# Attention on TensorE: values of two key tiles on two halves of the columns, weights summed beside

## The chip, the cores and the metric

The kernel runs on one NeuronCore of a Trainium2 chip. A core has five engines with their own instruction streams: TensorE (PE) multiplies matrices into PSUM, VectorE (DVE), ScalarE (ACT) and GpSimd (POOL) work element by element, SyncE (SP) issues DMAs. They wait for each other through semaphores. The metric is the device time of one execution in microseconds (us); the kernel before takes 3555.32 us, the median of three runs (3553.36 to 3558.95).

## The reference

Two layers of a model over 1024 latent tokens and 256 context tokens. Each layer projects its input, runs four mixers side by side (a gated linear recurrence called mLSTM, attention, and two state-space mixers), projects their outputs back and ends with a feed-forward part. The change touches the attention alone, and there what stands behind the projections, the product of weights and values and the softmax's denominator:

```python
def attend(q, k, v):
    s = jnp.einsum('bqhd,bkhd->bhqk', q, k).astype(jnp.float32) * scale
    p = jax.nn.softmax(s, axis=-1).astype(v.dtype)
    return jnp.einsum('bhqk,bkhd->bqhd', p, v)
...
yc = attend(qc, kc, vc).reshape(bsz, Tc, W_GROUP)
...
k_all = jnp.concatenate([kl, kc], axis=1)
v_all = jnp.concatenate([vl, vc], axis=1)
```

There are 4 heads with 96 features for the scores and 64 for the values. Context queries see the 256 context keys, latent queries all 1280 keys.

## The kernel before

Activations lie feature-major: 128 features on the partitions, tokens along the row. Tokens come in groups t0 = 0 (256 context tokens), 256 and 768 (512 latent tokens each); the last layer leaves the first group out as queries. Dense products run in float32r, a form of float32 that PE takes in one pass, three times with split operands (L242 to L244, a_pkn among them for the keys); products marked float32 take two passes, and the trace shows each pass as an instruction of its own.

Attention (class MLA) first builds values and keys. `values` makes `vt`, the values of a 128-token tile, token-major, with a block of ones between the two heads of a pair. `attend` goes over two head pairs, the two heads of each, and the groups of queries. For a head and a group it goes over the key tiles, 10 for latent queries and 2 for context queries: three float32r products give the scores of 128 keys and up to 512 queries in a PSUM bank (pst, L934 to L936), ACT takes the exponential into a tile E (L938), and one float32 product of 128 columns (L939) adds to the bank po: 64 columns are the values, the other 64 are ones, so that po holds the weighted values on one half of its partitions and the sums of the weights on the other. Over both layers there are 160 such key tiles of 512 queries and 8 of 256. At the group's end ACT copies both halves out (L941, L942); after the second head of a pair DVE takes the reciprocal (L944), POOL multiplies (L945), and the result goes to DRAM.

Between these steps `extra()` puts in other work by a written plan: steps of the mLSTM mixer (`cell`, products L740, L745, L753, L778, the norm m_w and m_h on POOL at L773 and L774) and parts of the modulation vectors (L151, narrow products of 32 columns on the four quarters of PE's columns). `scores` makes the next head's keys and each query's largest score (L903, reduced on DVE at L904). The program is written in this order, but a scheduler with a model of the engines then sets the order in which each engine's instructions stand; every engine starts its own in that order.

PSUM has 8 banks: 2 for dense products (pd), 3 (pa) for attention's po and pst, 3 (pb) for the other strand. L702 (mLSTM states, ahead of attention) are float32 products of 64 columns whose outputs go alternately to partitions 0 to 63 and 64 to 127 of a tile. L183 (norms) are products of 32 columns.

Of the kernel before, what the change touches and what calls it, by code (L numbers as in the profile page):

```python
# [15 lines left out]
P = 128  # L16
# [10 lines left out]
# order of the 128-column tiles of w_in  # L27
# [3 lines left out]
# columns of the per-layer vector pack  # L31
# [24 lines left out]
# before attend, then before and after each group  # L56
# [7 lines left out]
class Kern:  # L64
# [10 lines left out]
    # ------------------------------------------------------------------ setup  # L75
    def setup(self):
# [34 lines left out]
        # two banks for the dense products, and three for each of two strands of other work  # L111
# [4 lines left out]
    def few(self):  # L116
        """the dense products keep to their two banks"""
        self.cycle, self.turn = [self.pd], 0

    def many(self):  # L120
        """the dense products take those of the second strand too"""
        self.cycle, self.turn = [self.pd, self.pb, self.pb, self.pd, self.pb], 0
# [6 lines left out]
    # --------------------------------------------------------- modulation vectors  # L129
# [7 lines left out]
    def mod(self, l, tiles_, ws, pool, bank=None):  # L137
        """c @ w_mod + b for some of the 48 tiles of 128 columns: the vectors are the stationary operand, with
        two tiles of rows on each of the four column groups."""
# [32 lines left out]
    # --------------------------------------------------------------------- norms  # L172
    def rstd(self, tiles, nfeat, n, pool, name, bufs=2, out=None, sqs=None):
        """1/sqrt(mean of squares over the features) for n tokens, on every partition."""
# [24 lines left out]
    def split(self, src, hi, lo, eng=None):  # L199
        """hi = src in float32r, lo = src - hi (exact)."""  # L200
        nc = self.nc
        nc.scalar.copy(hi, src)  # L202
        (eng or nc.gpsimd).tensor_tensor(lo, src, hi.bitcast(F32), OP.subtract)  # L203

    def norm_apply(self, l, which, k, x, rb, act, t0, n, pool):
        """act(hi, lo)[k][:, t0:t0+n] = x*rb*(1+scale)+shift."""
# [15 lines left out]
    # --------------------------------------------------------------------- dense  # L222
# [14 lines left out]
    def dense_acc(self, ps, whi, wlo, ahi, alo, ks, start=True, stop=True):  # L237
        """ps += sum_k w[k]^T a[k], three float32r passes. whi/wlo/ahi/alo: callables k -> AP."""
# [16 lines left out]
    def dense_late(self, srcs, act, early, late, chunks, evacs, pool, names):  # L255
        """dense for some tiles of columns, first over the rows that are there, then over those that come late"""
# [24 lines left out]
def pieces(t0, n):  # L281
    """cut a token range at the end of the context"""
    if t0 < TC < t0 + n:
        return [(t0, TC - t0), (TC, t0 + n - TC)]
    return [(t0, n)]


def ppos(t):
    """position of a token in a row padded with one zero before, between and behind"""
    return t + 1 if t < TC else t + 2  # L290
# [6 lines left out]
# ------------------------------------------------------------------------ gates  # L297
class Gates:
    """Per-token scalars of the two gated mixers, token-major [128, direction, chunk, head]."""

    def __init__(self, K, l, misc, keep, pool):
# [14 lines left out]
        # softplus of -f and of dt: max(z, 0) + log1p(exp(-|z|))  # L316
# [22 lines left out]
        # L[d, 0] = log forget gate, L[d, 1] = dt * A  # L339
# [34 lines left out]
    def mlstm(self, keep, pool):  # L374
# [12 lines left out]
        # running maximum of a within each chunk, along the direction's time  # L387
# [13 lines left out]
        # m over the chunks: m <- max(m, cmax) + total, from zero, in each direction's order  # L401
# [5 lines left out]
        def orders(dst, src, inv):  # L407
            # src [p, d, (c h)], dst [p, d, h, 11]
# [40 lines left out]
        # decay by head pair: the first 64 partitions carry the even head of a pair, the others the odd one  # L449
# [8 lines left out]
class Expo:  # L458
    """E[s, h, t] = exp(bias[s, h] + row[t, h]) for s at or before t in direction d, else 0. The exponent is a product
    of bfloat16 matrices: bias and row come in three exact parts each."""  # L460

    def __init__(self, K, l, name, bias, row, pool):
        """bias, row: [P, 2, 40] contiguous, token-major; row None: minus the bias"""
# [60 lines left out]
# -------------------------------------------------------------------------- SSD  # L524
def cslice(c):
    """columns of a 128-token chunk in a row that has one spare column behind the context"""
    t = c * P + (1 if c >= TC // P else 0)
    return slice(t, t + P)


def nexts():
    """nexts[d][c]: the chunk whose starting state chunk c completes in direction d"""
    return [{o[i]: o[i + 1] for i in range(NCH - 1)} for o in ORDER]


class SSD:
    """states(): convolution and the state before each chunk; outputs(): the rest. src(i): the six tiles x, B, C before the
    convolution, DRAM. zsrc: silu(z), DRAM. keep: holds the states."""

    def __init__(self, K, l, g, src, zsrc, oc, keep):  # L540
# [4 lines left out]
        # [n, chunk, group, direction, (head, p)]: state before the chunk  # L545
        self.S = keep.tile([P, NCH, 2, 2, P], F32, name=n("S"))
        # by chunk: B and C feature-major, x token-major
# [55 lines left out]
    def outputs(self, pb, y_put):  # L603
# [5 lines left out]
        for t0, w in groups:  # L609
            yz = pb.tile([P, 2, 512], F32, tag="yz", name=n(f"yz{t0}"))  # L610
            for c in range(t0 // P, (t0 + w) // P):
# [9 lines left out]
                px = K.pa.tile([P, 2, 2, 2, 64], F32, tag="m", name=n(f"px{c}"))      # [t, group, direction, head, p]  # L621
# [34 lines left out]
def conv3(nc, dst, src, w0, w1, w2, bias, n):  # L656
    """dst[0..n) = w0*src[0..n) + w1*src[1..n+1) + w2*src[2..n+2) + bias; the weights are per-partition scalars."""
# [8 lines left out]
# ------------------------------------------------------------------------ mLSTM  # L666
# [6 lines left out]
def mlstm_states(K, l, g, src, pool, tmp):  # L673
    """src(tile): DRAM, two feature-major tiles each of q, k (already times 1/8), v, sigmoid(o).
    Returns the state before each chunk and the values, token-major with a one behind each head, DRAM."""
# [3 lines left out]
    # state before each chunk, rows (head of the pair, dim): [., chunk, pair, direction, e|n]  # L679
# [36 lines left out]
def mlstm(K, l, g, src, oc, states, pool, y_put):  # L716
# [3 lines left out]
    # queries of the four heads, the rows of the other head of the pair zero  # L720
# [7 lines left out]
    for ci, c in enumerate(oc):  # L728
# [7 lines left out]
        u = pool.tile([P, 2, 4, 65], F32, tag="u", name=n(f"u{c}"), bufs=3)      # [t, direction, head, e|n]  # L736
        for q in range(2):
            px = K.psm.tile([P, 2, 2, 65], F32, tag="m", name=n(f"px{c}{q}"))      # [t, odd, direction, e|n]
# [46 lines left out]
# -------------------------------------------------------------------------- MLA  # L785
def latent_norms(K, l, src, dst, pool, groups_kv, groups_q):
    """rmsnorm of the compressed keys and values, dst[0], and of the compressed queries, dst[1:3]"""
# [12 lines left out]
class MLA:  # L800
    """queries(), values(): queries, values and keys; attend(): the rest. src(tile, i), lat: DRAM, feature-major."""
# [10 lines left out]
    def latents(self, pq):  # L812
        """loads ahead of queries()"""
# [5 lines left out]
    def queries(self, late, pool):  # L819
        K, l, n, lat, pq, ws = self.K, self.l, self.n, self.lat, self.pq, self.ws  # L820
        nc, A = K.nc, K.A
        # late holds what the last head needs too
# [19 lines left out]
    def values(self, late, pool, pk):  # L842
# [3 lines left out]
        vt = self.vt = late.tile([P, NCH, 2, 192], F32, name=n("vt"))       # values of a pair of heads with ones between  # L846
# [12 lines left out]
        # values, token-major  # L859
        wv = pk.tile([P, 256], F32, name=n("wv"))  # L860
        nc.sync.dma_start(wv, A["w_uv"][l])
        nc.gpsimd.memset(vt[:, :, :, 64:128], 1.0)
        for c in range(NCH):
            ps = K.acc(n(f"pv{c}"))
            nc.tensor.matmul(ps[:, :256], kvf[:, c * P:c * P + P], wv, start=True, stop=True)
            psv = ps[:, :256].rearrange("p (a h e) -> p a h e", a=2, h=2)
            for o in range(2):
                nc.scalar.copy(vt[:, c, :, 128 * o:128 * o + 64], psv[:, :, o])
        # rope part of the keys, on partitions 64-127 twice (it meets q*cos and swapped q*sin)
# [11 lines left out]
        # row 96 takes the largest score off  # L881
# [3 lines left out]
    def scores(self, h, pool):  # L885
        """keys of a head, and the largest score of each query, from the leading halves"""
# [24 lines left out]
    def attend(self, pool, epool, y_put, extra):  # L911
        K, groups, n = self.K, self.groups, self.n
        nc, vt = K.nc, self.vt
        scale = 96 ** -0.5
        self.scores(0, pool)
        for hp in range(2):
            ys = {}
            for ho in range(2):
                h = 2 * hp + ho
                kh, kl, qh, ql = self.kh[ho], self.kl[ho], self.qh[h], self.ql[h]  # L920
                if h < 3:
                    self.scores(h + 1, pool)
                for t0, w in groups:
# [4 lines left out]
                    # sums over the keys: the weighted values on one half of the partitions, the weights on the other  # L928
                    po = K.psm.tile([P, 512], F32, tag="m", name=n(f"po{h}{t0}"))
                    kts = range(2) if t0 < TC else range(NCH)  # L930
                    for kt in kts:
                        ks = slice(kt * P, kt * P + P)
                        ps = K.psm.tile([P, 512], F32, tag="m", name=n(f"pst{h}{t0}{kt}"))
                        nc.tensor.matmul(ps[:, :w], kh[:97, ks], qh[:97, t0:t0 + w], start=True, stop=False)  # L934
                        nc.tensor.matmul(ps[:, :w], kh[:96, ks], ql[:96, t0:t0 + w], start=False, stop=False)
                        nc.tensor.matmul(ps[:, :w], kl[:96, ks], qh[:96, t0:t0 + w], start=False, stop=True)  # L936
                        E = epool.tile([P, 512], F32, tag="E", name=n(f"E{h}{t0}{kt}"), bufs=3)
                        nc.scalar.activation(E[:, :w], ps[:, :w], AF.Exp, scale=scale)  # L938
                        nc.tensor.matmul(po[:, :w], vt[:, kt, hp, 64 * ho:64 * ho + P], E[:, :w], start=kt == 0, stop=kt == kts[-1])  # L939
                    me, ot = slice(64 * ho, 64 * ho + 64), slice(64 - 64 * ho, 128 - 64 * ho)  # L940
# [892 lines left out]
```

## Time and profile before

| what | value |
|---|---|
| runs | 3553.36, 3555.32, 3558.95 us |
| span of the profiled execution | 3550.2 us (its time outside the span is not given) |
| PE busy | 96% of the span |
| DVE, ACT, POOL busy | 48%, 31%, 25% |
| attention, layer 0 | 592 to 870 us |
| attention, layer 1 | 2448 to 2690 us |

The profile is of one execution; its times are in us from the start of the span, and Lnn is a line of the kernel. Products on PE are pipelined and their ends are modelled, so the time that a product costs is better read from the distance between starts than from its own length. Of a piece of several merged instructions the length goes from the first one's start to the last one's end.

### The profile page before, as it was taken

To read this page: it belongs to the slowest core of one execution; us is meant where nothing else is said; L and a number is where in the kernel's file an instruction comes from. 1 tells how busy PE (TensorE), PEld (TensorE's weight loads), DVE (VectorE), ACT (ScalarE), POOL (GpSimd) and SP (SyncE) were. 2 spreads that over 40 slices of the span, in tenths; PEclk is the share of its full clock that TensorE was granted. 3 is DMA by queue.
4 is the path that set the end of the run, shared out by engine and by line. 5 is a ranking of instruction groups with operands and counts; after the bars stand their busy time and mean duration, and the time that the engine had idled before them with its cause. 6 is when DMAs were issued, how large, how long until landed. Compare 5 with 4: busy or idle time off the path is not lost. (4 is left out here: it accounts for less than half of the span.)

```text
span 3550.2 us, 48986 instructions
## 1 busy us (share of the span) xinstructions
PE 3418.2 (96%) x19154; PEld 2795.2 (79%) x19186; DVE 1708.2 (48%) x3597; ACT 1106.9 (31%) x1885; POOL 889.9 (25%) x1061
## 2 busy tenths in 40 slices
PE   8899998999999999999999999998999999999998
PEld 6888995676768888888887889985666688888885
DVE  6857727554365486333323563636633432232333
ACT  4224534334242211111223324533333312212222
POOL 1922424011033222222221011331110223323321
PEclk9899998999999999999999999998999999999999
DMA  5577533345111121111112655542153111111111
GB/s 200 166 205 229 156 119 113 110 140 212 65 46 62 54 90 72 36 36 36 42 40 81 162 166 164 142 150 67 60 204 107 42 42 54 53 42 54 48 46 62
DMA packets 264904, 352.84 MB, mean 99 GB/s; under 512 B 89240, under 2 KB 190304, under 8 KB 264672
## 3 DMA queue, kind: packets, MB, share of 16 engines
q1 hardware_dynamic: 168148, 265.90, 23.5%
q10 hardware_dynamic: 96524, 83.81, 7.5%
q8 instruction: 151, 2.47, 0.3%
q14 instruction: 81, 0.66, 0.1%
HBM read 266.09 MB, written 83.52 MB: 98 GB/s over the span
## 5 line engine op out<-in xcount | busy, mean ns | idle before, releaser
L1601 DVE SCALAR_TENSOR_TENSOR x<-pd,modv,x 128x512 f32<-128x512 f32 (+1 forms) x448 | 299.8, 687 | 233.6 <-PE pd L244 233.2
L242 PE MATMUL pd<-fh,wh_d 128*128 128x512 f32 (+1 forms) x896 | 325.3, 369 | 9.3 <-ACT fh L202 5.7
L242 PE MATMUL ps_g<-hb,wh_g 128*128 128x512 f32 (+1 forms) x880 | 326.0, 370 | 3.2 <-ACT hb L214 2.2
L244 PE MATMUL ps_g<-hb,wl_g 128*128 128x512 f32 (+1 forms) x880 | 324.4, 369 | 2.5 <-POOL wl_g L203 2.5
L243 PE MATMUL pd<-fl,wh_d 128*128 128x512 f32 (+1 forms) x896 | 326.0, 367 | 0.7 <-POOL fl L203 0.7
L244 PE MATMUL pd<-fh,wl_d 128*128 128x512 f32 (+1 forms) x896 | 325.5, 368 | 0.0
L242 PE MATMUL ps_u<-hb,wh_u 128*128 128x512 f32 (+1 forms) x880 | 325.4, 370 | 0.0
L243 PE MATMUL ps_g<-hb,wh_g 128*128 128x512 f32 (+1 forms) x880 | 325.1, 369 | 0.0
L243 PE MATMUL ps_u<-hb,wh_u 128*128 128x512 f32 (+1 forms) x880 | 324.7, 369 | 0.0
L244 PE MATMUL ps_u<-hb,wl_u 128*128 128x512 f32 (+1 forms) x880 | 324.3, 369 | 0.2 <-POOL wl_u L203 0.2
L662 DVE SCALAR_TENSOR_TENSOR cv<-gp,vec,cv 128x1281 f32<-128x1281 f32 (+1 forms) x44 | 72.6, 1651 | 476.8 <-ACT cv L659 476.8
L242 PE MATMUL ps_in<-ha,wh_in 128*128 128x384 f32 (+3 forms) x688 | 218.3, 326 | 13.5 <-ACT st L1426 13.5
L203 POOL TENSOR_TENSOR wl_u<-wr_u,wh_u 128x1024 fp32r<-128x1024 f32 x44 | 105.5, 2397 | 481.7 <-ACT wh_u L202 481.7
L243 PE MATMUL ps_in<-ha,wh_in 128*128 128x384 f32 (+3 forms) x688 | 222.4, 323 | 0.0
L244 PE MATMUL ps_in<-ha,wl_in 128*128 128x384 f32 (+3 forms) x688 | 221.2, 322 | 0.0
L242 PE MATMUL ps_in<-hb,wh_in 128*128 128x256 f32 (+1 forms) x704 | 212.7, 305 | 0.8 <-ACT hb L214 0.6
L244 PE MATMUL ps_in<-hb,wl_in 128*128 128x256 f32 (+1 forms) x704 | 212.8, 303 | 0.0
L243 PE MATMUL ps_in<-hb,wh_in 128*128 128x256 f32 (+1 forms) x704 | 212.5, 302 | 0.2 <-DVE hb L215 0.2
L242 PEld LDWEIGHTS pd<-fh,wh_d 128*128 128x128 f32 x896 | 169.1, 189 | 45.8 <-DVE x L1601 7.4
L202 ACT CAST wh_u<-wr_u 128x1024 fp32r<-128x1024 f32 x44 | 46.3, 1051 | 502.4 <-PE pd L243 436.5
L242 PEld LDWEIGHTS ps_g<-hb,wh_g 128*128 128x128 f32 x880 | 166.2, 189 | 36.4 <-ACT hb L214 3.5
L243 PEld LDWEIGHTS pd<-fl,wh_d 128*128 128x128 f32 x896 | 169.4, 189 | 31.9 <-issue 1.7
(509 smaller groups left out, 7691.2 us busy)
## 6 DMA issues: line engine op xcount, KB each, us to landing
wm<-in_w_mod SPq DMA_DIRECT2D x96, 512.0 KB
wr_in<-in_w_in SPq DMA_DIRECT2D x44, 512.0 KB
wr_g<-in_w_up SPq DMA_DIRECT2D x44, 512.0 KB
wr_u<-in_w_up SPq DMA_DIRECT2D x44, 512.0 KB
wr_d<-in_w_down SPq DMA_DIRECT2D x44, 512.0 KB
wr_out<-in_w_out SPq DMA_DIRECT2D x32, 512.0 KB
PF<-st ACTq DMA_DIRECT2D x100, 128.0 KB
PF<-st ACTq DMA_DIRECT2D x60, 192.0 KB
```

The costliest lines, as they stand in the source:

```text
L202: nc.scalar.copy(hi, src)
L203: (eng or nc.gpsimd).tensor_tensor(lo, src, hi.bitcast(F32), OP.subtract)
L242: nc.tensor.matmul(ps, whi(k), ahi(k), start=start and i == 0, stop=False)
L243: nc.tensor.matmul(ps, whi(k), alo(k), start=False, stop=False)
L244: nc.tensor.matmul(ps, wlo(k), ahi(k), start=False, stop=stop and i == len(ks) - 1)
L662: nc.vector.scalar_tensor_tensor(dst, src[:, 0:n], w0, dst, OP.mult, OP.add)
L1601: nc.vector.scalar_tensor_tensor(v, ps, K.modv[l][:, 8 * part + m, c:c + 1], v, OP.mult, OP.add)
```

## The change

`vt` loses its ones and holds four heads of 64 columns. In `attend` the key tiles are taken two at a time. Their two value products are 64 columns wide and go to the two halves of po, the even key tile to partitions 0 to 63, the odd one to 64 to 127, both accumulated over the pairs; in the program they stand behind the score products of the next pair. The sums of the weights are formed apart: POOL adds the E tiles of the even key tiles, DVE those of the odd ones, DVE adds the two (tot), and one full-width float32 product with a matrix of ones (L976, `finish`) gives the sum over the partitions; it is put off until the next group's second pair. At the group's end ACT copies one half of po and DVE adds the other to it. E has six buffers instead of three.

```diff
-        vt = self.vt = late.tile([P, NCH, 2, 192], F32, name=n("vt"))       # values of a pair of heads with ones between
+        vt = self.vt = late.tile([P, NCH, 4, 64], F32, name=n("vt"))
...
-        nc.gpsimd.memset(vt[:, :, :, 64:128], 1.0)
         for c in range(NCH):
             ps = K.acc(n(f"pv{c}"))
             nc.tensor.matmul(ps[:, :256], kvf[:, c * P:c * P + P], wv, start=True, stop=True)
-            psv = ps[:, :256].rearrange("p (a h e) -> p a h e", a=2, h=2)
-            for o in range(2):
-                nc.scalar.copy(vt[:, c, :, 128 * o:128 * o + 64], psv[:, :, o])
+            nc.scalar.copy(vt[:, c], ps[:, :256].rearrange("p (h e) -> p h e", h=4))
...
-                    po = K.psm.tile([P, 512], F32, tag="m", name=n(f"po{h}{t0}"))
-                    kts = range(2) if t0 < TC else range(NCH)
-                    for kt in kts:
-                        ks = slice(kt * P, kt * P + P)
...
-                        E = epool.tile([P, 512], F32, tag="E", name=n(f"E{h}{t0}{kt}"), bufs=3)
-                        nc.scalar.activation(E[:, :w], ps[:, :w], AF.Exp, scale=scale)
-                        nc.tensor.matmul(po[:, :w], vt[:, kt, hp, 64 * ho:64 * ho + P], E[:, :w], start=kt == 0, stop=kt == kts[-1])
...
+                    po = bank(f"po{h}{t0}")
+                    nk = 2 if t0 < TC else NCH
+                    sums, old = [None, None], None
+
+                    def values(k0, es):
+                        for i, E in enumerate(es):
+                            nc.tensor.matmul(po[64 * i:64 * i + 64, :w], vt[:, k0 + i, h], E[:, :w], start=k0 == 0, stop=k0 + 2 == nk)
+
+                    for k0 in range(0, nk, 2):
+                        es = []
+                        for i in range(2):
...
+                            E = epool.tile([P, 512], F32, tag="E", name=n(f"E{h}{t0}{kt}"), bufs=6)
+                            nc.scalar.activation(E[:, :w], ps[:, :w], AF.Exp, scale=scale)
+                            es.append(E)
+                        if old:
+                            values(*old)
+                        if k0 == 2:
+                            settle()
+                        old = k0, es
+                        eng = (nc.gpsimd, nc.vector)
+                        for i, E in enumerate(es):
+                            if k0:
+                                new = epool.tile([P, 512], F32, tag=f"S{i}", name=n(f"S{i}{h}{t0}{k0}"), bufs=1) if k0 == 2 else sums[i]
+                                eng[i].tensor_tensor(new[:, :w], sums[i][:, :w], E[:, :w], OP.add)
+                                sums[i] = new
+                            else:
+                                sums[i] = E
+                    values(*old)
+                    tot = epool.tile([P, 512], F32, tag="S", name=n(f"S{h}{t0}"), bufs=1)
+                    nc.vector.tensor_tensor(tot[:, :w], sums[0][:, :w], sums[1][:, :w], OP.add)
                     nc.scalar.copy(r[me, :w], po[ot, :w])
-                    nc.scalar.copy(y[me, :w], po[me, :w])
...
+                    nc.vector.tensor_tensor(y[me, :w], po[me, :w], r[me, :w], OP.add)
+
+                    def finish(h=h, ho=ho, t0=t0, w=w, y=y, r=r, me=me, hp=hp, tot=tot):
+                        ps = bank(f"pr{h}{t0}")
+                        nc.tensor.matmul(ps[:, :w], K.ones, tot[:, :w], start=True, stop=True)
+                        nc.scalar.copy(r[me, :w], ps[me, :w])
+                        if ho:
+                            nc.vector.reciprocal(r[:, :w], r[:, :w])
+                            nc.gpsimd.tensor_tensor(y[:, :w], y[:, :w], r[:, :w], OP.mult)
+                            y_put(2 + hp, 1, y[:, None, :w], t0, w)
+
+                    settle()
+                    later.append(finish)
                     extra()
+        settle()
```

The scheduler sets the order anew. The next two pieces are of PE in layer 0 (a0), head 0, queries from 768 on; a name like E07683 is head 0, queries 768, key tile 3, and po0768 the bank of that head and group. Before, around the value products of key tiles 3 and 4:

```order
L939 MATMUL a0_po0768_7771<-a0_E07683_7797,a0_vt_6556 128x512
L934 MATMUL a0_pst07685_7807<-a0_qh0_6644,a0_kh0_6552 128x512
L935 MATMUL a0_pst07685_7807<-a0_ql0_6648,a0_kh0_6552 128x512
L936 MATMUL a0_pst07685_7807<-a0_qh0_6644,a0_kl0_6554 128x512
L939 MATMUL a0_po0768_7771<-a0_E07684_7804,a0_vt_6556 128x512
L934 MATMUL a0_pst07686_7814<-a0_qh0_6644,a0_kh0_6552 128x512
L935 MATMUL a0_pst07686_7814<-a0_ql0_6648,a0_kh0_6552 128x512
L936 MATMUL a0_pst07686_7814<-a0_qh0_6644,a0_kl0_6554 128x512
```

Each value product, 128 columns wide in its weights, stands between the score products of later key tiles.

The same place in the changed program, from the value product of key tile 3 to that of key tile 4:

```order
L941 MATMUL a0_po0768_7777<-a0_E07683_7800,a0_vt_6556 64x512
L900 MATMUL a0_pm120_7336<-a0_kh1_6553,a0_qh1_6634 128x512
L905 MATMUL a0_pmr10_7332<-cst_60,a0_mx1_7323 1x128
L949 MATMUL a0_pst07685_7817<-a0_qh0_6633,a0_kh0_6552 128x512
L950 MATMUL a0_pst07685_7817<-a0_ql0_6637,a0_kh0_6552 128x512
L951 MATMUL a0_pst07685_7817<-a0_qh0_6633,a0_kl0_6554 128x512
L949 MATMUL a0_pst07686_7827<-a0_qh0_6633,a0_kh0_6552 128x512
L950 MATMUL a0_pst07686_7827<-a0_ql0_6637,a0_kh0_6552 128x512
L951 MATMUL a0_pst07686_7827<-a0_qh0_6633,a0_kl0_6554 128x512
L941 MATMUL a0_po0768_7777<-a0_E07684_7815,a0_vt_6556 64x512
```

Key tile 4 is the even half of its pair; its odd partner, key tile 5, stands four rows further down. The two halves are parted by full-width products, and so are those of tiles 2 and 3.

PE at the start of the same group in the changed program, with the first pair and the product with ones (pr0256) of the group before:

```order
L949 MATMUL a0_pst07683_7796<-a0_qh0_6633,a0_kh0_6552 128x512
L950 MATMUL a0_pst07683_7796<-a0_ql0_6637,a0_kh0_6552 128x512
L951 MATMUL a0_pst07683_7796<-a0_qh0_6633,a0_kl0_6554 128x512
L900 MATMUL a0_pm100_7324<-a0_kh1_6553,a0_qh1_6634 128x256
L941 MATMUL a0_po0768_7777<-a0_E07680_7782,a0_vt_6556 64x512
L941 MATMUL a0_po0768_7777<-a0_E07681_7788,a0_vt_6556 64x512
L900 MATMUL a0_pm110_7328<-a0_kh1_6553,a0_qh1_6634 128x256
L976 MATMUL a0_pr0256_7804<-a0_S0256_7653,ones_68 128x512
L941 MATMUL a0_po0768_7777<-a0_E07682_7794,a0_vt_6556 64x512
```

Here the halves of key tiles 0 and 1 stand next to each other, and tile 2's stands alone behind the product with ones.

POOL in layer 0 where attention begins, before (m_w and m_h are the norm of the mLSTM's outputs by chunk):

```order
L773 TENSOR_TENSOR m0_w0_6987<-m0_v0_6984,mhalf_70 128x4
L774 TENSOR_TENSOR m0_h0_6980<-m0_h0_6980,m0_w0_6987 128x256
L773 TENSOR_TENSOR m0_w1_7057<-m0_v1_7054,mhalf_70 128x4
L774 TENSOR_TENSOR m0_h1_7050<-m0_h1_7050,m0_w1_7057 128x256
L773 TENSOR_TENSOR m0_w2_7127<-m0_v2_7124,mhalf_70 128x4
```

The same place in the changed program, with the sums S0 of the even key tiles:

```order
L964 TENSOR_TENSOR a0_S002562_7599<-a0_E02560_7574,a0_E02562_7586 128x512
L773 TENSOR_TENSOR m0_w0_6976<-m0_v0_6973,mhalf_70 128x4
L774 TENSOR_TENSOR m0_h0_6969<-m0_h0_6969,m0_w0_6976 128x256
L964 TENSOR_TENSOR a0_S002562_7599<-a0_S002562_7599,a0_E02564_7607 128x512
L964 TENSOR_TENSOR a0_S002562_7599<-a0_S002562_7599,a0_E02566_7623 128x512
L964 TENSOR_TENSOR a0_S002562_7599<-a0_S002562_7599,a0_E02568_7639 128x512
L773 TENSOR_TENSOR m0_w1_7046<-m0_v1_7043,mhalf_70 128x4
L964 TENSOR_TENSOR a0_S007682_7807<-a0_E07680_7782,a0_E07682_7794 128x512
```

The additions stand between the steps of the norm, in one queue with them.

## Rows read from the trace of the kernel before

**Rows 1.** The page: the span, busy time, and the granted clock in 40 slices.

```profile
span 3550.2 us, 48986 instructions
PE 3418.2 (96%) x19154; PEld 2795.2 (79%) x19186; DVE 1708.2 (48%) x3597; ACT 1106.9 (31%) x1885; POOL 889.9 (25%) x1061
...
PEclk9899998999999999999999999998999999999999
```

**Rows 2.** Busy time by engine in the two attention stretches.

```profile
core 0: us, PE busy (x) PEld busy (x) DVE busy (x) ACT busy (x) POOL busy (x), PEclk, DMA share, GB/s
592.00:870.00 278.00, 275.20 (x1910) 191.55 (x1919) 145.44 (x343) 109.32 (x201) 32.00 (x35) 0.99 0.41 140
2448.00:2690.00 242.00, 237.57 (x1421) 154.34 (x1427) 116.74 (x252) 90.79 (x160) 25.34 (x26) 1.00 0.31 107
```

**Rows 3.** Waits of PE, layer 0's stretch, then layer 1's: us in total, times, longest.

```profile
PE a_po L939 <- ACT a_E L938: 0.6, 2, 0.3
...
PE ps_out L242 <- ACT hb L202: 1.9, 1, 1.9
PE a_po L939 <- ACT a_E L938: 0.7, 1, 0.7
```

**Rows 4.** Timeline of PE, two key tiles of attention in layer 0.

```profile
start us, us, engine line op out<-in xcount [idle before <-releaser]
640.63 1.02 PE L939 MATMUL a_po<-a_E,a_vt 128*128 128x512 f32 x2
...
642.20 1.02 PE L939 MATMUL a_po<-a_E,a_vt 128*128 128x512 f32 x2
...
643.30 0.40 PE L935 MATMUL a_pst<-a_ql,a_kh 96*128 96x512 f32 x1
643.54 0.40 PE L936 MATMUL a_pst<-a_qh,a_kl 96*128 96x512 f32 x1
```

**Rows 5.** Timeline of PE around L702.

```profile
526.20 0.34 PE L244 MATMUL ps_in<-ha,wl_in 128*128 128x384 f32 x1
526.47 0.66 PE L702 MATMUL m_pu<-m_vw,m_kt 128*64 128x130 f32 x8
527.07 0.44 PE L691 MATMUL m_pt<-cst,m_lk 128*128 128x128 f32 x2
527.34 0.38 PE L691 MATMUL m_pt<-cst,m_lv 128*128 128x128 f32 x2
```

**Rows 6.** Timeline of PE: L183 on four quarters.

```profile
25.32 1.04 PE L183 MATMUL ss_n<-sq_n,ones 128*32 128x512 f32 x8
```

**Rows 7.** Timeline of PE: L183 on one quarter.

```profile
199.84 0.28 PE L242 MATMUL ps_in<-ha,wh_in 128*128 128x256 f32 x1
200.05 1.04 PE L183 MATMUL ss_ln<-sq_ln,ones 128*32 128x512 f32 x2
201.03 0.39 PE L243 MATMUL ps_in<-ha,wh_in 128*128 128x256 f32 x1
201.25 0.28 PE L244 MATMUL ps_in<-ha,wl_in 128*128 128x256 f32 x1
```

**Rows 8.** Timeline of PE around the keys' products a_pkn.

```profile
576.83 0.36 PE L244 MATMUL a_ps_q<-a_cqh,wl_a_q 128*128 128x424 f32 x1
577.02 0.36 PE L242 MATMUL a_pkn<-a_kvh,a_wkh 128*64 128x432 f32 x1
...
577.62 0.36 PE L242 MATMUL a_ps_q<-a_cqh,wh_a_q 128*128 128x424 f32 x1
```

**Rows 9.** Groups by line, layer 0: xcount | busy us, mean ns | idle us before.

```profile
L945 POOL TENSOR_TENSOR a_y<-a_y,a_r 128x512 f32<-128x512 f32 x3 | 3.9, 1286 | 33.2 <-DVE a_r L944 33.2
...
L750 DVE TENSOR_TENSOR m_pT<-m_pg,Em 128x512 f32<-128x512 f32 x20 | 13.8, 688 | 7.9 <-ACT Em L517 7.8
L944 DVE RECIPROCAL a_r<-a_r 128x512 f32<-128x512 f32 x3 | 10.0, 3347 | 0.6 <-ACT a_r L941 0.6
...
L868 ACT COPY a_vt<-a_pv 128x128 f32<-128x128 f32 x20 | 4.2, 268 | 6.1 <-PE a_pv L865 6.0
```

More of the change, by code (lines that the diff above doesn't have):

```diff
@@ L914, in attend, with settle @@
         scale = 96 ** -0.5
+        bank = lambda s: K.psm.tile([P, 512], F32, tag="m", name=n(s))
+        later = []
+        def settle():
+            while later:
+                later.pop(0)()
         self.scores(0, pool)
@@ L920, in attend @@
                 kh, kl, qh, ql = self.kh[ho], self.kl[ho], self.qh[h], self.ql[h]
+                me, ot = slice(64 * ho, 64 * ho + 64), slice(64 - 64 * ho, 128 - 64 * ho)
                 if h < 3:
@@ L927, in attend @@
                     y, r = ys[t0]
-                    po = K.psm.tile([P, 512], F32, tag="m", name=n(f"po{h}{t0}"))
-                    kts = range(2) if t0 < TC else range(NCH)
-                    for kt in kts:
-                        ks = slice(kt * P, kt * P + P)
[L933 to L936, printed above, removed]
-                        E = epool.tile([P, 512], F32, tag="E", name=n(f"E{h}{t0}{kt}"), bufs=3)
-                        nc.scalar.activation(E[:, :w], ps[:, :w], AF.Exp, scale=scale)
-                        nc.tensor.matmul(po[:, :w], vt[:, kt, hp, 64 * ho:64 * ho + P], E[:, :w], start=kt == 0, stop=kt == kts[-1])
@@ L940, in attend @@
-                    me, ot = slice(64 * ho, 64 * ho + 64), slice(64 - 64 * ho, 128 - 64 * ho)
-                    nc.scalar.copy(r[me, :w], po[ot, :w])
-                    nc.scalar.copy(y[me, :w], po[me, :w])
-                    if ho:
-                        nc.vector.reciprocal(r[:, :w], r[:, :w])
-                        nc.gpsimd.tensor_tensor(y[:, :w], y[:, :w], r[:, :w], OP.mult)
-                        y_put(2 + hp, 1, y[:, None, :w], t0, w)
+                    po = bank(f"po{h}{t0}")
@@ new lines, in attend @@
+                    nk = 2 if t0 < TC else NCH
[6 more added lines that the diff above has]
+                        for i in range(2):
+                            kt = k0 + i
+                            ks = slice(kt * P, kt * P + P)
+                            ps = bank(f"pst{h}{t0}{kt}")
+                            nc.tensor.matmul(ps[:, :w], kh[:97, ks], qh[:97, t0:t0 + w], start=True, stop=False)
+                            nc.tensor.matmul(ps[:, :w], kh[:96, ks], ql[:96, t0:t0 + w], start=False, stop=False)
+                            nc.tensor.matmul(ps[:, :w], kl[:96, ks], qh[:96, t0:t0 + w], start=False, stop=True)
+                            E = epool.tile([P, 512], F32, tag="E", name=n(f"E{h}{t0}{kt}"), bufs=6)
[14 more added lines that the diff above has]
+                                sums[i] = E
```

## Prediction

> **What bounds the kernel now.** I read the page first: TensorE (PE) is busy for 96% of the span, and the row of its granted clock stands at 9 in nearly all of the 40 slices [rows 1]. Then the two stretches in which attention runs, one for each layer: 278 us and 242 us, PE busy for 275.2 and 237.6 of them at a granted clock of 0.99 and 1.00; VectorE (DVE) for 145.4 and 116.7; GpSimd (POOL) for 32.0 and 25.3 [rows 2]. Busy time of pipelined products proves little, so next come PE's waits there. The longest entry is 1.9 us on a product of the next stage; on the exponentials of this change it waits 0.6 us in layer 0 and 0.7 in layer 1 [rows 3]. So in these 520 us the time is the sum of what PE streams. Last comes the timeline of one key tile [rows 4]: a tile starts at 640.63 us and the next at 642.20, 1.57 us. The three float32r products of the scores follow each other at 0.23 to 0.24 us, which leaves 0.86 us for the one float32 product L939 with the values, its two passes over 512 columns of 0.43 us. With 160 key tiles of 512 queries and 8 of 256, L939 costs 160 x 0.86 + 8 x 0.43 = 141 us of the kernel.
>
> **The change, part by part.** (1) Two value products on two halves of the columns. That halves run together is in this trace: L702, also float32 and 64 columns wide, puts 8 passes of 130 columns between 526.47 us and the next product at 527.07, 0.60 us [rows 5]. At L939's rate a pass of 130 takes 0.11 us; one after another they would need 0.87, two at a time 0.44. L183 shows the same on quarters: 8 passes of 512 columns in a piece of 1.04 us, and 2 passes elsewhere in a piece of 1.04 us too [rows 6, 7]. So two neighbouring halves cost 0.86 instead of 1.72 us.
>
> But they must be neighbours. PE starts its products in the order of its program, and a full-width product between two halves needs all columns. The order of the changed kernel parts most pairs: its 168 value products stand in 138 uninterrupted stretches, 109 of one product, 28 of two, one of three. Twenty-nine products then run beside a neighbour, one of them 256 wide: 28 x 0.86 + 0.43 = 24.5 us saved. All 84 pairs would have saved 70.5.
>
> (2) Each change between full-width and narrow float32 products costs time. At the rate of the scores a float32r product of 384 columns takes 0.18 us, but from the one ahead of L702 to L702 it is 0.27, 0.09 more; L702's 0.60 us is 0.16 more than its paired passes; and the full-width L691 behind it takes 0.27 us for two passes worth 0.22, 0.05 more [rows 4, 5]. In and out together: 0.30 us. At L183 [rows 7], whose neighbours of 256 columns are worth 0.12: 0.21 before it (0.09 more), 0.98 instead of 0.86 in it (0.12), 0.22 for the float32r product behind it (0.10): 0.31. L702 has the longer load of 64 columns and L183 the dearer float32r successor; most of the changed products have both, so I take 0.32. In the changed order 130 stretches begin behind a full-width product and 122 end before one (the others touch products that are narrow already): 126 round trips, 126 x 0.32 = 40.3 us. PE hardly waits here, so nothing hides them. Bounds: the highest that I can build from these rows is 0.35 us, L702's terms with L183's 0.10 at the end in place of 0.05, 44 us. The lowest is nothing: L242 to L244 of the keys (a_pkn) are 64 wide and stand between full-width products at an even 0.19 to 0.20 us [rows 8]. These are float32r; the changed product is float32 like L702, so I stay with 0.32.
>
> The Trainium skill (TensorEngine Tiling (Array Packing), Key Properties) says that changing the tiling mode, not just the tile, drains TensorE; that speaks against this change. Rows 5 and 7 agree, with some 0.3 us for a change there and back; the float32r rows 8 do not. The page has no price; by its rule with rows 5 the sum is the one below, by rows 8 it would be 40 us lower.
>
> (3) One product with ones (L976) for each head and group of queries: 16 of 512 columns and 4 of 256, full width, float32: 16 x 0.86 + 4 x 0.43 = +15.5 us on PE, hidden by nothing. It stands well behind the work it needs, by my count from the order and these durations 2.7 us of PE work behind the last scores of its group in one case, 5.9 us or more in the other 19.
>
> (4) The weights' sums. POOL gets 64 additions of 128x512, priced at L945's 1.29 us: 83 us. DVE gets the same 64 at L750's 0.69, 20 totals, and 20 additions out of PSUM, which I price at 0.69 too: 72 us [rows 9]. With [rows 2] POOL goes from 57 to 140 and DVE from 262 to 334 busy us of 520, 64%. ScalarE loses 20 copies of the values and gets 20 of the sums, no change. These additions cost nothing while PE has work queued: the value products now run a pair later than their exponentials. Without that cover each late sum would hold PE for up to a reciprocal of 3.35 us [rows 9] that stands ahead of it on DVE. Behind a waiting addition on POOL stand the norms m_w and m_h of the mLSTM cells, and the E buffers of the next exponentials, six now instead of three. I take 0, and 20 us as the other end. The change also ends the 1.3 us that PE waits for exponentials: -1.3.
>
> (5) The values' layout (vt) saves 20 of 40 ScalarE copies of 0.27 us [rows 9] and a memset, ahead of attention, where ScalarE is not what PE waits for most; I count 0 (at most the 5 us of 20 copies).
>
> Sum: -24.5 + 40.3 + 15.5 - 1.3 = +30.0 us. On the profiled span of 3550.2 us that is 3580.2. Of what lies around the span only the difference to the runs is shown: the median of 3555.3 is 5.1 above it. I forecast **3585 us**, 0.8% slower. A measurement of this kernel can tell about 0.2%, 7 us, from no change: faster is below 3548, slower above 3562.
>
> **The rivals.** *A. All pairs run together*, the change does what it says: 84 round trips of 0.32 (27 us), -70.5 and +15.5: 28 us less, 3527. For it: halves do overlap [rows 5]. Against it: it needs two halves next to each other, and the order has 29. The Trainium skill (TensorEngine Tiling (Array Packing), Theoretical Speedup) allows up to twofold where 64 columns suffice; as a price for all pairs that would be this rival. 4%.
> *B. The width changes free of charge*, as in rows 8: then -24.5 + 15.5 - 1.3 = -10 us, 3545, faster. It decides where a round trip costs under 0.03 us. Against it stand both float32 places, 0.30 and 0.31. 8%.
> *C. The sums come late*: a full DVE queue holds PE at the group ends, 10 reciprocals at some 2 us each: 20 us more, 3605. For it: DVE and POOL take their work in order, and the norm's steps and reciprocals stand between the additions. Against it: DVE has a third of its time left, and L976 stands late. 10%.
> *D. Neighbouring halves do not overlap*, since both write one PSUM bank: +24.5, 3610. L702 does the same into one tile, so 3%.
>
> **How the numbers follow.** The forecast has 75%, with an own range of 3570 to 3600 (a round trip between 0.22 and 0.35, up to 8 us of new waits). Faster: A, and nearly all of B: 11%. Between 3548 and 3562, a round trip of 0.03 to 0.14 us: 4%. Slower: 85%. The range leaves out A, B and what is above C, with a little room on both sides: 3560 to 3608.
>
> **What would show it.** Right: two L941 products in a row whose passes start within 10 ns, and a lone L941 that keeps its two passes of 0.43; about 0.1 us more than the spacing before it and behind it, and 0.1 in the product that follows; both attention stretches longer, together by about 30 us, with all else unchanged; 20 L976 of 0.86 us that wait for nothing. Wrong: if L941 follows L951 at the usual spacing, B holds; if PE waits for DVE or POOL in attention grow beyond 10 us, C; if far more than 29 products start beside a neighbour, A.

## The result, and the profile after

The changed kernel takes 3591.1 us (median of 4 runs, 3585.4 to 3593.8), the kernel before beside it 3554.9. The ratio is 1.010, interval [1.0086, 1.0115]: 1% slower. The profiled execution's span is 33.2 us longer. The page of the changed kernel:

```profile
span 3583.4 us, 49268 instructions
PE 3457.2 (96%) x19226; PEld 2766.4 (77%) x19226; DVE 1784.8 (50%) x3701; ACT 1106.9 (31%) x1865; POOL 977.3 (27%) x1123
...
PEclk9999998999999999999999999998999999999999
```

TensorE is busy 39.0 us longer than in [rows 1] and idle 5.8 us less (span minus busy: 126.2 for 132.0). The busy time by stretch, first to last attention product of each layer, answers to [rows 2]:

```profile
core 0: us, PE busy (x) PEld busy (x) DVE busy (x) ACT busy (x) POOL busy (x), PEclk, DMA share, GB/s
587.00:882.00 295.00, 291.09 (x1938) 172.49 (x1938) 183.44 (x398) 113.71 (x207) 80.28 (x76) 0.98 0.40 132
...
2464.00:2720.00 256.00, 252.28 (x1445) 137.62 (x1444) 147.47 (x298) 91.14 (x159) 68.96 (x59) 1.00 0.30 101
```

The two stretches grew by 17 and 14 us, 31 of the 33. PE is as full as before, so the new time is work and not waiting. Its waits in layer 0, for [rows 3]:

```profile
PE a_pm L900 <- DVE a_mx L901: 1.9, 3, 0.8
PE a_pm L900 <- ACT a_qh L906: 0.7, 1, 0.7
PE a_po L941 <- ACT a_E L953: 0.4, 1, 0.4
```

No entry of TensorE's waits there names the additions L964 or L970, and the products with ones wait for nothing. The timeline shows the new prices, for [rows 4] (columns: start us, us, engine, line, operation, count):

```profile
649.24 0.39 PE L950 MATMUL a_pst<-a_ql,a_kh 96*128 96x512 f32 x1
649.47 0.40 PE L951 MATMUL a_pst<-a_qh,a_kl 96*128 96x512 f32 x1
649.80 1.07 PE L941 MATMUL a_po<-a_E,a_vt 128*64 128x512 f32 x2
650.80 0.38 PE L740 MATMUL m_px<-m_C,m_qz 128*128 128x130 f32 x1
...
653.26 0.40 PE L900 MATMUL a_pm<-a_kh,a_qh 96*128 96x512 f32 x1
653.59 1.08 PE L941 MATMUL a_po<-a_E,a_vt 128*64 128x512 f32 x4
654.60 0.39 PE L949 MATMUL a_pst<-a_qh,a_kh 97*128 97x256 f32 x1
654.82 0.28 PE L950 MATMUL a_pst<-a_ql,a_kh 96*128 96x256 f32 x1
...
659.07 1.12 PE L976 MATMUL a_pr<-a_S,ones 128*128 128x512 f32 x2
660.03 0.78 PE L753 MATMUL m_pi<-m_lvt,m_pT 128*128 128x65 f32 x6
```

A lone half (x2 passes, at 649.80) starts 0.33 us behind the score product ahead of it, which costs 0.23 elsewhere, and the next product starts 1.00 us later, not 0.86. A pair (x4 passes, at 653.59) takes 1.01 us to the next start: twice the work in the same time. Behind it, L949 with 256 columns takes 0.22 us instead of 0.12. So a round trip from full width to narrow and back costs 0.10 + 0.15 + 0.10 at its dearest. The product with ones L976, which stands right behind a narrow product, takes 0.96 us to the next start, the 0.86 that were priced and the 0.10 of the way out.

### The profile page after: what moved, and what is told of

The parts are those of the page before. It is cut to its first block, busy times and chain, and to the rows that moved or that the text cites. A ratio compares the mean times of both kernels' runs of the same rounds, so it can differ in the third digit from the quotient of the medians.

```text
span 3583.4 us, 49268 instructions
## 1 busy us (share of the span) xinstructions
PE 3457.2 (96%) x19226; PEld 2766.4 (77%) x19226; DVE 1784.8 (50%) x3701; ACT 1106.9 (31%) x1865; POOL 977.3 (27%) x1123
## 5 line engine op out<-in xcount | busy, mean ns | idle before, releaser
L244 PEld LDWEIGHTS pd<-fh,wl_d 128*128 128x128 f32 x896 | 169.8, 190 | 32.1 <-issue 4.2
```

What stands on the lines that cost most here:

```text
L244: nc.tensor.matmul(ps, wlo(k), ahi(k), start=False, stop=stop and i == len(ks) - 1)
```

## Experiments

To compare traces, each span is cut into three sums. Idle is span minus PE's busy time on the page. The clock's part is half of PE's busy time in the stretches granted 0.50 (the lower level, 1.2 GHz), summed over the trace's records of the clock: a score product takes 0.42 us there (753.70 to 754.12 in the full width run) and 0.23 at full clock, so that half is a round figure for 45%, which moves no entry by more than 2.3 us. The rest is what PE streams, and only that is what the prediction's prices speak of: 0.86 saved for each neighbour, 0.32 for each round trip, 0.86 for each product with ones. All as differences to the kernel before, us; "priced" uses each program's own order. The three sums are those of one profiled execution of each kernel, the medians are of all its runs:

| kernel | median | interval of the ratio | span | idle | clock | streamed | priced |
|---|---|---|---|---|---|---|---|
| changed | 3591.1 | 1.0086 to 1.0115 | +33.2 | -5.8 | +10.5 | +28.5 | +31.3 |
| adjacent halves | 3531.0 | 0.9918 to 0.9958 | -26.4 | +0.7 | +3.5 | -30.6 | -31 |
| full width | 3583.7 | 1.0058 to 1.0098 | +35.4 | +0.6 | +17.8 | +17.0 | +15.5 |
| one half | 3615.2 | 1.0156 to 1.0190 | +63.2 | +5.5 | -0.9 | +58.6 | +56 |
| three pairs | 3540.7 | 0.9950 to 0.9976 | -13.6 | +16.2 | +8.7 | -38.5 | -44 |
| no additions | 3586.2 | 1.0078 to 1.0107 | +32.1 | -10.1 | +5.6 | +36.6 | +35 |
| float32r, 128 | 3471.4 | 0.9760 to 0.9788 | -82.1 | +0.2 | -2.8 | -79.5 | -87 |
| float32r, 64 | 3477.1 | 0.9773 to 0.9798 | -76.8 | -2.1 | +12.0 | -86.7 | -87 |
| paired ones, pieces | 3547.8 | 0.9976 to 0.9999 | -7.7 | +17.7 | +13.9 | -39.3 | -39.5 |
| before, float32r | 3477.9 | 0.9757 to 0.9796 | -73.1 | +4.6 | +14.4 | -92.1 | -102 |
| pieces only | 3532.8 | 0.9916 to 0.9949 | -23.5 | +2.7 | +3.9 | -30.1 | -31 |
| pairing only | 3547.8 | 0.9968 to 0.9990 | +3.1 | +20.1 | +22.4 | -39.4 | -37 |
| two pairs | 3541.2 | 0.9950 to 0.9980 | -11.4 | +15.1 | +9.2 | -35.7 | -41 |

The clock differs nearly as much from run to run of one kernel as between kernels. The kernel before was granted 0.977 to 0.983 over 39 runs (0.981 in the profiled one), the changed kernel 0.978 to 0.979 over its four, adjacent halves 0.981 in the profiled run of 3525.7 us and 0.974 in one of 3541.2. A few us in the clock column are therefore not shown to be the program's own.

**Adjacent halves.** The half whose exponential comes last is issued first.

```diff
-for i, E in enumerate(es):
+for i, E in ((1, es[1]), (0, es[0])):
     nc.tensor.matmul(po[64 * i:64 * i + 64, :w], vt[:, k0 + i, h], E[:, :w], ...)
```

> The changed kernel with the two value products of a pair issued in the reverse order (the later key tile first). Both write one tile and stay in order, so the second half can no longer start ahead: the 168 products now stand in 83 uninterrupted stretches, 82 of two and one of four, where there were 138. Theory (overlap of neighbours 0.86 us a pair, round trip of width 0.32 us, product with ones 0.86 us): against the kernel before -70.5 for 84 pairs, +24 for 74 round trips from full width and back (the other stretches touch narrow products), +15.5 for the ones, -1.3: -32, that is 3523 us, 68 below the changed kernel. If halves do not overlap (rival D), only the 52 round trips fewer are gained: 3574. If the width changes are free and the loss came from waits for the sums (rivals B and C together), 3545 at best. If order does not matter, 3591.

Measured 3531.0, 60 us below the changed kernel and 24 below the kernel before. All 84 pairs now overlap, with the price that the lone pair had in the changed kernel:

```profile
646.69 0.40 PE L900 MATMUL a_pm<-a_kh,a_qh 96*128 96x512 f32 x1
647.02 1.08 PE L941 MATMUL a_po<-a_E,a_vt 128*64 128x512 f32 x4
648.03 0.39 PE L949 MATMUL a_pst<-a_qh,a_kh 97*128 97x256 f32 x1
```

PE streams 30.6 us less than before, as the prices say (-31); the miss of 8 us against the forecast is idle time, the clock, and 2 us more between the median and the span than in the kernel before. Rival D falls, and with it the claim that order does not matter: the overlap was lost in the order alone.

**Full width.** Here, with one half and in the two float32r versions of the change, y also comes out of po in one copy, without the addition of two halves.

```diff
-nc.tensor.matmul(po[64 * i:64 * i + 64, :w], vt[:, k0 + i, h], ...)
+nc.tensor.matmul(po[:, :w], vt[:, k0 + i, 2 * hp:2 * hp + 2], ...)
```

> The changed kernel with its value products 128 columns wide (the values of both heads of a pair in one product, 64 of the columns unused), so there is no width change and no overlap; the sums of the weights on GpSimd and VectorE and the product with ones stay. Theory: against the kernel before only the product with ones, +15.5, and the waits for exponentials, -1.3: 3569 us, 22 below the changed kernel. Rival (width changes free, the sums hold TensorE): what the changed kernel lost stays and the overlap of 24.5 us is lost too: 3616. Rival C alone (sums cost 20 us): 3589.

Measured 3583.7, 15 above the theory; close to rival C by its time, but not by its cause. PE's idle time is the kernel before's (+0.6) and its streaming is +17.0 for 15.5. What is new is the clock. VectorE's timeline, then PE's:

```profile
742.75 0.43 DVE L741 TENSOR_TENSOR m_u<-m_px,gm_wi 128x260 f32<-128x260 f32 x1
743.10 3.34 DVE L978 RECIPROCAL a_r<-a_r 128x512 f32<-128x512 f32 x1
746.36 0.10 DVE L163 TENSOR_TENSOR modv<-pm,vec 128x8 f32<-128x8 f32 x1
746.38 1.27 DVE L901 TENSOR_REDUCE a_mx<-a_pm 128x1 f32<-128x512 f32 x2
```

```profile
744.77 0.38 PE L514 MATMUL em<-maskb,identb 128*128 128x512 bf16 x1
747.11 0.38 PE L900 MATMUL a_pm<-a_kh,a_qh 96*128 96x256 f32 x1 [1.95 <-DVE a_mx L901]
```

The maxima L901 stand behind a reciprocal in VectorE's queue, PE waits 1.95 us for them, and right behind that the granted clock is at 0.50 for 17.1 us:

```profile
742.00:748.20 6.20, 4.03 (x26) 3.07 (x26) 5.87 (x8) 1.18 (x2) 2.87 (x3) 1.00 0.63 225
748.20:765.30 17.10, 16.42 (x91) 10.85 (x89) 6.75 (x18) 2.98 (x5) 1.26 (x1) 0.50 0.18 58
```

In it the score products start 0.42 us apart:

```profile
753.70 0.63 PE L949 MATMUL a_pst<-a_qh,a_kh 97*128 97x512 f32 x1
754.12 0.63 PE L950 MATMUL a_pst<-a_ql,a_kh 96*128 96x512 f32 x1
```

PE is busy for 16.42 of these 17.1 us at about half its pace, so some 8 us are lost behind a wait of 2. The runs on record fit: those granted 0.979 took 3572.9 and 3580.9 us, those granted 0.976 took 3586.4 and 3587.6, the last of which is the profiled one. The same happens once in the float32r version of the kernel before (a reciprocal at 2496.14, 3.62 us of wait, clock 0.50 from 2500.4 for 17 us). It does not follow each such wait: 2.1 us at 727.7 in the first experiment left the clock alone.

**One half.** 

```diff
-nc.tensor.matmul(po[64 * i:64 * i + 64, :w], vt[:, k0 + i, h], E[:, :w], start=k0 == 0, stop=k0 + 2 == nk)
+nc.tensor.matmul(po[me, :w], vt[:, k0 + i, h], E[:, :w], start=k0 + i == 0, stop=k0 + i + 1 == nk)
```

> The changed kernel with all value products on one half of the columns, one accumulation, so that neighbours wait for each other; the width changes are as many (141 stretches for 138). Theory: the 24.5 us that 29 neighbours save are lost and three round trips are added: 3591 + 24.5 + 1 = 3616 us. Rival D (halves do not overlap anyway): 3591. Against the full width version of this group, with the same overlap of none, it shows the price of the width changes alone: 126 times 0.32, 40 to 46 us by the theory, nothing by rival B.

Measured 3615.2. Two neighbours on the same half now take 1.86 us:

```profile
609.85 1.93 PE L941 MATMUL a_po<-a_E,a_vt 128*64 128x512 f32 x4
611.71 0.70 PE L975 MATMUL a_pr<-a_S,ones 128*128 128x256 f32 x2
```

Overlap is due to the halves. Against the full width run PE streams 41.6 us more: that is the price of about 126 round trips, 0.33 us each. Rival B falls.

**Three pairs in a stretch, and two.** The value products of several pairs are issued together (the list is walked from its end, so the last exponential lets all go):

```diff
+part.append((k0, es))
+if len(part) == 3:            # 2 in the other run
+    old, part = part, []
-E = epool.tile([P, 512], F32, tag="E", ..., bufs=6)
+E = epool.tile([P, 512], F32, tag="E", ..., bufs=12)      # 8
```

> The changed kernel with reversed order as in the first run of this group, and the value products of up to three pairs of key tiles issued in one stretch, 12 buffers for the exponentials in place of 6: 38 stretches (18 of four, 14 of six, 6 of two) instead of 83. Theory: 34 round trips instead of 74, 13 us less than the reversed order alone: 3510 us. If borders are free, the same as that run. If the sums or the exponentials now come late (20 groups end with a longer run of value products), some 10 to 20 us above it.

> As the run with three pairs in a stretch, with two (four products) and 8 buffers: 53 stretches in place of 83, 7 us less of streaming than the first experiment. Theory: 3531 - 7 = 3524 us if attention's last rows come in time; rival (a longer delay of the value products makes the last rows late, as with three pairs, 16 us of idle): 3540.

Measured 3540.7 and 3541.2. Streaming falls by 8 and 5 us against adjacent halves (13 and 7 were expected, 13 and 10 as priced by the order), but 14 to 16 us of idle time come back, the rival's side. Where they come from is told below with the paired ones.

**No additions.** 

```diff
-eng[i].tensor_tensor(new[:, :w], sums[i][:, :w], E[:, :w], OP.add)
-sums[i] = new
+sums[i] = E
...
-nc.vector.tensor_tensor(tot[:, :w], sums[0][:, :w], sums[1][:, :w], OP.add)
+nc.vector.tensor_scalar(tot[:, :w], sums[0][:, :w], 1.0, None, OP.add)
```

> The changed kernel without the 64 additions on GpSimd and the 64 on VectorE: the total that goes to the product with ones is taken from one tile of exponentials alone (plus one), so the denominators are left incomplete; everything on TensorE stays. The order of its products comes out a little different: 26 neighbours instead of 29 and some 3 round trips more, worth +4 us. Theory (the additions lie beside TensorE's work and cost nothing): 3595 us. Rival C (late sums hold TensorE for 20 us): 3575. If the additions cost TensorE only through its clock, the time in the lower clock goes from the 153 us of the changed kernel to the 135 of the kernel before, and the time to about 3587.

Measured 3586.2, beside 3591.1 of the changed kernel; the intervals of the ratios overlap. It streams 8 us more, as its order is another, and has 4 us less idle time and 5 us less of the clock. So between these two executions the additions account for at most some 9 us, through short waits and the clock, and not for rival C's 20; with a clock that differs that much from run to run, whether they cost anything is not shown.

**Values in float32r, 128 and 64 columns wide.** 

```diff
-vt = self.vt = late.tile([P, NCH, 4, 64], F32, ...)
+vt = self.vt = late.tile([P, NCH, 4, 64], F32R, ...)
-E = epool.tile([P, 512], F32, ...)
+E = epool.tile([P, 512], F32R, ...)
```

The 64 wide version also writes po[:64, :w] with vt[:, k0 + i, h].

> The full width version (values 128 columns wide) with the exponentials and the values held in float32r, so that a value product is one pass of 0.235 us in place of two of 0.43; the last bits of both are left out. Theory: 160 x 0.625 + 8 x 0.30 = 102 us less on TensorE than the full width version with float32, whose time without its stretches of lower clock was some 3570: 3468, or 3480 if those stretches come again. It is the base of the next run and tells the theories apart only together with it.

> The same in float32r with the values 64 columns wide, on one half of the columns, in 144 stretches between products of full width (143 in the 128 column version). Theory, by the float32r products a_pkn of the kernel before, which are 64 wide and stand among others at the usual spacing: no price of a width change, the same time as the 128 column version within 8 us. Rival (the price belongs to the width and not to the float32 product): 126 round trips of 0.32, 40 us more.

Measured 3471.4 and 3477.1; the narrow one streams 7 us less and loses 15 to the clock. In it a 64 column product stands among the others without a gap:

```profile
640.29 0.39 PE L900 MATMUL a_pm<-a_kh,a_qh 96*128 96x512 f32 x1
640.52 0.40 PE L941 MATMUL a_po<-a_E,a_vt 128*64 128x512 f32 x1
640.76 0.28 PE L949 MATMUL a_pst<-a_qh,a_kh 97*128 97x256 f32 x1
640.88 0.29 PE L950 MATMUL a_pst<-a_ql,a_kh 96*128 96x256 f32 x1
```

0.23 us before it, 0.24 for it, 0.12 for the next. The price of a width change belongs to the float32 product, not to the 64 columns alone, as [rows 8] against [rows 5] had it; why, these runs do not show.

**Paired ones with reciprocals in pieces, and each alone.** On top of adjacent halves:

```diff
-nc.tensor.matmul(ps[:, :w], K.ones, tot[:, :w], start=True, stop=True)
+for o in (1, 0):
+    nc.tensor.matmul(ps[64 * o:64 * o + 64, :w], K.ones[:, :64], tots[t0, o][:, :w], start=True, stop=True)
...
-nc.vector.reciprocal(r[:, :w], r[:, :w])
+for c in range(0, w, P):
+    nc.vector.reciprocal(r[:, c:c + P], r[:, c:c + P])
```

> A version meant to beat both kernels: the reversed order of the first experiment; the products with ones of the two heads of a pair, 64 columns each, next to each other on the two halves; and the reciprocal in pieces of 128 columns so that VectorE's queue is never held for 3.35 us. Theory: ten products with ones of 0.86 (two of them 0.43) run beside another, -7.7, and up to five round trips more, +1: 3531 - 7 = 3524 us. If the waits of TensorE behind the reciprocals and the lower clock after them go too, 3515. Rival (DVE's reciprocals are no matter and what counts is the number of stretches): 3530.

> The first experiment (reversed order) with one edit more: the reciprocal in pieces of 128 columns. TensorE streams the same by its order (+2 us). Theory after the paired version came out at 3548 with 18 us more idle TensorE than in the kernel before, 11 of them ahead of the output projection: pairing the products with ones made the last rows of attention late, the pieces did nothing: 3531 us here. Rival (the pieces, which take their turn one by one, did it): 3545.

> The first experiment with the other edit alone: the products with ones of two heads next to each other, the reciprocal whole. TensorE streams 5 us less than there. Theory (pairing makes the last rows late): 3540 to 3548 us. Rival (pieces did it): 3526.

Measured 3547.8 together, 3532.8 with the pieces alone, 3547.8 with the pairing alone. The pieces do nothing; pairing streams 9 us less and still loses 17: against adjacent halves its two traces have 17 and 19 us more idle time and 10 and 19 us more of the clock. The one long wait is at the output projection behind attention in layer 0. The DMA issues on SP, paired ones first, then adjacent halves (w_out comes in tiles of 0.5 MB, each x here is 2 MB):

```profile
858.36 0.33 SPq L230 DMA_DIRECT2D wr_out<-in_w_out  x1
860.05 2.61 SPq L1652 DMA_DIRECT2D yraw<-YD  x4
864.08 1.28 SPq L1656 DMA_DIRECT2D x<-in_x  x2
865.45 3.19 SPq L230 DMA_DIRECT2D wr_out<-in_w_out  x1
868.74 13.66 SPq L1652 DMA_DIRECT2D yraw<-YD  x5
```

```profile
864.26 0.33 SPq L230 DMA_DIRECT2D wr_out<-in_w_out  x1
865.21 1.28 SPq L1653 DMA_DIRECT2D x<-in_x  x2
866.59 4.96 SPq L1649 DMA_DIRECT2D yraw<-YD  x1
871.64 14.59 SPq L230 DMA_DIRECT2D wr_out<-in_w_out  x4
```

In both the loads of x stand between the sixth tile of w_out (858.36 and 864.26) and the seventh (865.45 and 871.64). With paired ones ScalarE, which splits the seventh tile, waits for it, and PE for ScalarE:

```profile
879.17 1.04 ACT L202 CAST wh_out<-wr_out 128x1024 fp32r<-128x1024 f32 x1 [12.40 <-DMA wr_out<-in_w_out]
```

```profile
868.81 0.39 PE L244 MATMUL ps_out<-hb,wl_out 128*128 128x512 f32 x1
880.57 0.80 PE L242 MATMUL ps_out<-hb,wh_out 128*128 128x256 f32 x2 [11.37 <-ACT hb L202]
```

The stretches, paired ones, then adjacent halves, show the DMA engines full in both (shares 1.01 and 0.95), but PE with work in one only:

```profile
865.30:880.50 15.20, 2.99 (x15) 2.17 (x15) 2.76 (x4) 2.71 (x6) 1.19 (x1) 0.72 1.01 363
```

```profile
864.20:880.50 16.30, 16.21 (x92) 14.28 (x93) 5.55 (x8) 2.42 (x3) 0.00 (x0) 1.00 0.95 349
```

Loads of x stand ahead of the seventh tile of w_out in the traces of all 14 kernels, so their order is not what sets the slow ones apart. What does is where the output projection stands. PE where its first products stand and at the last value products of attention, paired ones, then adjacent halves:

```profile
849.12 1.46 PE L941 MATMUL a_po<-a_E,a_vt 128*64 128x512 f32 x6
852.88 0.97 PE L242 MATMUL ps_out<-hb,wh_out 128*128 128x256 f32 x4
```

```profile
822.84 0.39 PE L242 MATMUL ps_out<-hb,wh_out 128*128 128x256 f32 x1
854.06 1.08 PE L941 MATMUL a_po<-a_E,a_vt 128*64 128x512 f32 x4
```

With paired ones no product of the output projection stands ahead of attention's last value product, with adjacent halves 72 do. None stand there in three pairs, two pairs, and pairing with and without pieces, and these four wait 9.0 to 12.3 us at this place; in the other ten 23 to 72 stand there, and the longest wait is 2.2 us. So "the last rows late" is not it: ScalarE waits for weights, and attention's last value product even starts earlier with paired ones (850.0 for 854.5 us). The new order puts the whole output projection behind attention, and TensorE runs out of it while the 4 MB pass. That the order causes the wait is argued from 14 traces; no kernel with the projection or the loads moved back was run.

**Before, in float32r.** The same two types in the kernel before, E with 6 buffers.

> The kernel before, its layout kept (64 columns of values beside 64 of ones, so no sums of weights and no product with ones), with the exponentials and the values in float32r and 6 buffers for the exponentials: the last bits of both are left out. Theory: 102 us less than the kernel before, 3452, and 16 us below the 128 column version of the change in float32r, since the product with ones (15.5 us) is not there. Rival: at 0.94 us of TensorE per key tile the exponentials come late, as 160 tiles wait some 0.1 us each: 3468.

Measured 3477.9, beside 3471.4 for the 128 column version with sums. PE streams 12.6 us less than that one, as 15.5 for the ones would have it, but has 17 us more from the clock and 4 from waits. Its rival, 3468, is nearer, but for a wrong reason: in layer 0 TensorE waits 0.6 us for exponentials and 7 us for the maxima, and the clock takes more than both. In streaming, all three float32r runs save 0 to 10 us less than priced; which product takes it is open.

## Why the prediction was right

- *The sum.* 3585 us was forecast, 3591.1 measured; +30.0 on the span, +33.2 found. PE's streaming, +28.5, is within 3 us of -24.5 + 40.3 + 15.5. The rest is the clock, +10.5, against -5.8 of idle time; the prediction had -1.3 for idle time and nothing for the clock. That the sum comes within 3.2 us of the measured one is in part luck: the clock, which it left out, offsets the 7 us by which streaming and idle time came out lower.
- *Neighbouring halves.* 28 pairs at the price of one: seen in the trace; with all 84 brought together, and the round trips that this saves, 60 us. The rival A was right about its size (3527 for 3531) and wrong only about what this kernel's order does.
- *Width changes.* 0.32 us was taken, 41.6 us for 126, 0.33 each, were measured by two kernels that differ in little else (full width and one half). The Trainium skill (TensorEngine Tiling (Array Packing), Key Properties) has TensorE drain when the tiling mode changes; the cost in the float32 runs agrees, the float32r run shows no such cost.
- *The products with ones.* +15.5 priced, +17.0 streamed in the full width run, which has nothing else new on PE.
- *The additions.* POOL's and DVE's busy time in the two stretches came to 149 and 331 us (140 and 334 forecast), and no wait of PE there names them. The zero for their cost may have been a little low: the version without them differs by 9 us in waits and clock, which is not clear of what the clock does from run to run.
- *Where it was off.* Nothing in the sum stood for the clock: the 14 profiled executions were granted the lower level for 128 to 192 us of their spans, which put from -3 to +22 us on the time against the kernel before. Runs of one kernel differ nearly as widely, so of the changed kernel's +10.5 an unknown part is the draw of the two profiled runs.

## What to carry to other kernels

Before narrow products are laid on two halves of the columns, read the order in which they will stand: the gain exists only where two stand together, and each lone one pays about 0.33 us for the way in and out in float32. Where the program is ordered by readiness, issue first the half whose input comes last; that one line was worth 60 us here. When TensorE is full, count what it streams, then look at what the new order does to loads and waits elsewhere: four versions that streamed less than adjacent halves lost it where the next stage's products no longer stood among attention's and TensorE ran dry behind a load of 4 MB.

## What the runs showed of the hardware

- A wait of TensorE of 2.0 and one of 3.6 us (busy for 4.0 of the 6.2 us and 11.5 of the 15 us around them) were each followed by 17 us at the lower clock, though PE was busy for 16 of them: the wait cost itself and some 8 us more. Another of 2.1 us was not.
- The granted clock is no constant of a program: 39 runs of the kernel before had 0.977 to 0.983, four of adjacent halves 0.974 to 0.981.
- Narrow float32r products among full-width ones cost no more than the usual spacing (0.23, 0.24, 0.12 us around one); narrow float32 products cost about 0.33 us a round trip.
- One pass of float32r in the value products takes the time to 3471 us with sums apart and 3478 with the ones in the values, 2.3 and 2.2% below the kernel before. Keeping float32, adjacent halves at 3531 are the fastest, ratio 0.994.
